# Starting weight tiles, slabs and loaded tiles at multiples of 1024 bytes in a one-core decoder step

## The chip, the core and the metric

The kernel runs on one core of a Trainium2 chip. The metric is the device time of one execution in microseconds (us). Work is spread over five engines that run side by side and wait for one another by semaphores: TensorE (PE, with its weight loads as PEld), VectorE (DVE), ScalarE (ACT), GpSimd (POOL) and SyncE (SP), which issues nearly all DMAs here. The on-chip memory is 128 partitions; a tile takes the same byte range in each of them, so "a tile begins at byte a" means byte a of every partition.

## The reference

One layer of a decoder step for 2048 prompt positions and 64 sample positions (8 sequences of 8), width 1024:

```python
hp = rmsnorm(xp, norm_mix_w[l])
mp, sr_p, sh_p = mixer(hp, pos_p, zero_ret, zero_hg, w_in[l], ...)   # projection, two chunked recurrences, gates, w_out
xp = xp + mp
hp = rmsnorm(xp, norm_ffn_w[l])
xp = xp + jnp.square(jax.nn.relu(hp @ w_up[l])) @ w_down[l]
y_prompt = rmsnorm(xp, final_norm_w)
```

The mixer projects 1024 columns to 8 x 512, runs retention (4 heads) and HGRN2 (4 heads) as chunked recurrences, normalises and gates each head, and multiplies by `w_out`. The samples take the same path from given states. All of it is float32, and the final states are outputs too.

## The kernel before

**Arithmetic.** A float32 product is made of three fp32r products: each operand is cut into a rounded part (`hi`, made by ScalarE with `copy`) and the rest (`lo`, made by VectorE with a subtraction), and TensorE adds hi x hi, hi x lo and lo x hi. Every such matmul goes through one helper, `matmul` at L1365, which also advances a clock of "ticks" on which the rest of the program is planned.

**Two stages.** The 2112 positions are cut into groups. The first stage ("mixing", to about 1115 us) takes groups of 640, 768 and 704 positions through norm, projection (`proj`), recurrences and part of the output projection; its wide matmuls stream half a group, 320, 384 or 352 columns, and the value projections (`values`) stream 256. The second stage ("feeding") takes three groups of 704 through the rest of the output projection and the MLP, whose products are made by a seven-product scheme (`up`, `down`); its matmuls all stream 352 columns.

**Tiles.** A "slab" is a tile of 768 float32 (3072 bytes), and 49 of them serve all activations; 4 tiles `ld` of the same size take loads, 6 tiles `w` of 4096 bytes hold weight parts as `hi` and `lo`, and tiles `raw` of 4096 bytes receive weights from memory, 4 in mixing and 9 in feeding. A group's half of 352 columns begins at byte 0 or at byte 1408 of its slab; a weight block of 128 columns begins at a multiple of 512 bytes of its `w` tile.

**What sets the addresses.** Pools are laid out one behind the other in the order in which `build` opens them: `cp` (the small constants `vec`, `ones`, `ones_r`, `eps`), `wp` (`w`), `sl` (`slab`), `ld` (`ld`), and behind these the pool of the stage, `mp` in mixing (`con`, `msk`, `raw`, `reset`, `S`, `AT`) and `rp` in feeding (`raw`). A tile takes a multiple of 32 bytes. So the length of the last small constant, `eps` at L454, moves the start of everything behind it. What it holds are two columns, the two epsilons of the norms, used as biases by ScalarE (L419).

**What sets the order.** Instructions stand in the order of the code and of the tick agenda; a pool's number of buffers sets how early a load can go out. None of that looks at an address.

Of the kernel before, what the change touches and what calls it, by code (L numbers as in the profile page):

```python
# [9 lines left out]
F32 = mybir.dt.float32  # L10
# [5 lines left out]
P = 128  # L16
# [14 lines left out]
LAG = 14  # L31
SOON = None
SLAB = 768
NSLAB = 49
NLD = 4
NRAW, NFRAW = 4, 9
# [158 lines left out]
class Kernel:  # L195
# [25 lines left out]
    def get(self, dt=F32):  # L221
        return self.sl.tile([P, SLAB], dt, tag="slab", name="slab")

# [5 lines left out]
    def load(self):  # L229
        return self.ld.tile([P, SLAB], F32, tag="ld", name="ld")  # L230

# [199 lines left out]
    def build(self):  # L431
        nc, tc, I = self.nc, self.tc, self.I
        with ExitStack() as ctx:
            cp = ctx.enter_context(tc.tile_pool(name="cp", bufs=1))
            self.wp = ctx.enter_context(tc.tile_pool(name="wp", bufs=3))
            self.sl = ctx.enter_context(tc.tile_pool(name="sl", bufs=NSLAB))
            self.ld = ctx.enter_context(tc.tile_pool(name="ld", bufs=NLD))
            self.dp = ctx.enter_context(tc.tile_pool(name="dp", bufs=1, space=bass.MemoryType.DRAM))
            self.w_next = self.w_load = self.w_use = 0
            self.columns, self.raws, self.tick_columns = 0, {}, TICK  # L440
            self.feeding = False
            self.ordered = True
            self.ahead = 2
            self.wts, self.second, self.kept = {}, {}, {}
            self.blocks = deque()
            self.mix_end = [0, 0]
            self.plan_stream()

            self.vec = cp.tile([P, NVEC], F32, name="vec")
            self.ones = cp.tile([P, P], F32, name="ones")  # L450
            self.ones_r = cp.tile([P, P], F32R, name="ones_r")
            nc.vector.memset(self.ones, 1.0)
            nc.vector.tensor_copy(self.ones_r, self.ones)
            eps = cp.tile([P, 2], F32, name="eps")  # L454
            nc.vector.memset(eps[:, 0:1], EPS)
            nc.vector.memset(eps[:, 1:2], EPS * DK)
            self.eps, self.eps_h = eps[:, 0:1], eps[:, 1:2]

            gs = self.groups(GROUPS)
            fs = self.feed_groups(gs)  # L460
            with ExitStack() as mixing:
                self.mixing_pools(mixing)
                self.mix_all(gs, fs[0])
            with ExitStack() as feeding:
                self.feeding_pools(feeding)
                self.feed_all(fs)
# [117 lines left out]
    def parts(self, src, n):  # L584

        t, half = self.getr(), SLAB // 2
        hi, lo = t[:, :n], t[:, half:half + n] if 2 * n <= SLAB else self.getr()[:, :n]
        self.nc.scalar.copy(hi, src)
# [1253 lines left out]
```

## Time and profile before

| | us |
|---|---|
| median of three runs (lowest, highest) | 2530.86 (2529.09, 2533.78) |
| the profiled execution | 2532.16 |
| its span, first to last instruction | 2530.4 |
| PE busy | 2498.1 (99%) |
| PEld busy | 2472.6 (98%) |
| DVE busy | 1855.8 (73%) |
| ACT busy | 1223.8 (48%) |

The profile is one execution. Its span is the time from the first instruction to the last; 1.8 us of its own time lie outside the span. A matmul's record lasts from its start to a modelled end, and records overlap, so the busy time of a group divided by its count, or the length of an unbroken run of matmuls divided by their number, tells what one of them takes on TensorE; the mean of one record does not. The granted clock of TensorE over the execution is 0.998 of its upper level of 2.4 GHz.

### The profile page before, as it was taken

The page shows a single profiled execution, that of the slowest core. Times are in us where ns is not written, and L with a number is a line of the kernel's source. Part 1 is how long each engine was busy: PE and PEld are TensorE (multiplying, and loading weights), DVE is VectorE, ACT ScalarE, POOL GpSimd, SP SyncE. Part 2 cuts the span into 40 slices and gives each one's busy share as a digit, 9 for nine tenths or more (in the row PEclk, how much of TensorE's full clock was granted, in tenths as well). Part 3 has the DMA queues.
Part 4 walks back from the last instruction along what each step waited for, and adds up shares of the span by engine and source line. Part 5 has one row for each costly group of instructions (what it writes and reads, how often), then busy time and mean ns, then how long its engine had stood idle before and what let it go on. Part 6 is the DMA issues. An engine that isn't in the chain of part 4 may idle for free.

```text
span 2530.4 us, 41661 instructions
## 1 busy us (share of the span) xinstructions
PE 2498.1 (99%) x16605; PEld 2472.6 (98%) x16605; DVE 1855.8 (73%) x2750; ACT 1223.8 (48%) x1769; POOL 26.4 (1%) x42
## 2 busy tenths in 40 slices
PE   8999999999999999999999999999999999999998
PEld 8999999999999999989999999999999999999998
DVE  7768866677867756656756997766599866758987
ACT  6546654345534445425444543554454445445544
POOL 0000000000000000000000000000000000000000
PEclk9999999999999999999999999999999999999999
DMA  6456685778798744484667654566766554667652
GB/s 214 150 202 233 228 298 177 238 267 294 274 330 297 280 135 145 152 286 165 190 202 250 232 187 160 178 186 192 220 237 218 172 199 153 187 191 244 206 182 71
DMA packets 185155, 532.83 MB, mean 211 GB/s; under 512 B 20736, under 2 KB 46080, under 8 KB 184960
## 3 DMA queue, kind: packets, MB, share of 16 engines
q1 hardware_dynamic: 184816, 530.14, 62.6%
q8 instruction: 131, 2.15, 0.3%
q14 instruction: 64, 0.52, 0.1%
q10 hardware_dynamic: 144, 0.02, 0.0%
HBM read 390.62 MB, written 138.67 MB: 209 GB/s over the span
## 4 chain that ended last, share of the span: by engine, by line
PE 93%; DMA 2%; DVE 2%; ACT 1%; issue 1%; SPq 0%; DVEq 0%; ACTq 0%
PE pj L1365 84%; PE mm L1062 1%; PE po L1244 1%; DMA raw<-w 1%; PE mm L1250 1%; PE po L1242 1%; PE mm L1119 1%; PE mm L595 1%; PE mm L594 1%; DMA s44S<-raw 1%; PE mm L1176 1%; PE po L933 1%; PE mm L992 1%; DVE slab L1023 0%; PE mm L1365 0%
## 5 line engine op out<-in xcount | busy, mean ns | idle before, releaser
L1365 PE MATMUL pj<-slab,w 128*128 128x352 f32 (+2 forms) x12696 | 2106.0, 324 | 10.3 <-ACT w L648 5.8
L1365 PEld LDWEIGHTS pj<-slab,w 128*128 128x128 f32 x12696 | 2028.1, 188 | 14.9 <-ACT w L648 5.8
L338 ACT CAST w<-raw 128x1024 fp32r<-128x1024 f32 x373 | 391.5, 1050 | 611.3 <-PE pj L1365 515.2
L360 DVE TENSOR_TENSOR w<-raw,w 128x1024 fp32r<-128x1024 f32 x373 | 455.0, 1222 | 116.3 <-ACT w L338 103.9
L1365 PE MATMUL pj<-w,slab 128*128 128x256 f32 x1632 | 225.9, 288 | 0.1
L1413 DVE TENSOR_TENSOR slab<-slab 128x704 fp32r<-128x704 f32 x216 | 187.6, 886 | 31.1 <-ACT slab L1409 27.5
L1365 PEld LDWEIGHTS pj<-w,slab 128*128 128x128 f32 x1632 | 205.6, 190 | 2.1 <-ACT slab L898 0.5
L1409 ACT CAST slab<-slab 128x704 fp32r<-128x704 f32 x216 | 163.1, 780 | 91.1 <-DVE slab L1420 86.1
L1629 DVE TENSOR_TENSOR slab<-pj,slab 128x704 f32<-128x704 f32 x166 | 146.9, 888 | 62.1 <-PE pj L1365 60.8
L296 DVE TENSOR_TENSOR raw<-raw 128x1024 f32<-128x1024 f32 x60 | 74.0, 1233 | 55.6 <-DMA raw<-w 53.7
L1420 DVE TENSOR_TENSOR slab<-slab 128x704 f32<-128x704 f32 x120 | 103.6, 885 | 0.0
L1557 DVE TENSOR_TENSOR ld<-pj,slab 128x704 f32<-128x704 f32 x63 | 56.1, 890 | 53.6 <-PE pj L1365 53.4
L1043 ACT ACTIVATE slab<-slab 128x640 f32<-128x640 f32 (+2 forms) x72 | 56.2, 781 | 72.4 <-DVE slab L1039 72.0
L1557 DVE TENSOR_TENSOR slab<-pj,slab 128x704 f32<-128x704 f32 x42 | 37.4, 891 | 64.9 <-PE pj L1365 64.9
L1063 DVE COPY_PREDICATED AT<-msk,mm 128x256 f32<-128x256 uint8 (+1 forms) x72 | 39.1, 545 | 40.0 <-PE mm L1062 31.2
L413 ACT CAST slab<-slab 128x704 fp32r<-128x704 f32 (+2 forms) x48 | 37.0, 778 | 37.9 <-DMA slab<-o 16.8
L419 ACT ACTIVATE slab<-mm,eps 128x384 f32<-128x384 f32 (+3 forms) x54 | 29.6, 551 | 52.8 <-PE mm L595 49.6
L1062 PE MATMUL mm<-slab 128*128 128x128 f32 x384 | 54.1, 274 | 0.0
L1244 PE MATMUL po<-slab,S 128*128 128x128 f32 x240 | 47.0, 283 | 4.7 <-DVE S L1257 4.6
L1062 PEld LDWEIGHTS mm<-slab 128*128 128x128 f32 x384 | 51.1, 191 | 0.0
L784 ACT COPY slab<-pj 128x384 f32<-128x384 f32 (+1 forms) x64 | 26.7, 466 | 49.4 <-PE pj L1365 47.3
L1327 ACT ACTIVATE slab<-po 128x384 f32<-128x384 f32 (+2 forms) x48 | 22.0, 459 | 56.4 <-PE po L1244 56.3
(187 smaller groups left out, 1991.8 us busy)
## 6 DMA issues: line engine op xcount, KB each, us to landing
raw<-w SPq DMA_DIRECT2D x253, 512.0 KB, 4.2
u<-ld SPq DMA_DIRECT2D x96, 352.0 KB, 4.4
slab<-u SPq DMA_DIRECT2D x96, 352.0 KB, 4.9
y<-slab SPq DMA_DIRECT2D x20, 352.0 KB, 2.9
ld<-x SPq DMA_DIRECT2D x16, 384.0 KB, 6.5
raw<-s44S SPq DMA_DIRECT2D x12, 512.0 KB, 3.9
raw<-s48S SPq DMA_DIRECT2D x12, 512.0 KB, 4.5
raw<-s52S SPq DMA_DIRECT2D x12, 512.0 KB, 3.7
```

The lines of the kernel that those rows point to most:

```text
L296: nc.vector.tensor_tensor(out=x[into], in0=x[a], in1=x[b], op=op)
L338: self.nc.scalar.copy(hi, raw)
L360: self.nc.vector.tensor_tensor(out=lo, in0=raw, in1=hi.bitcast(F32), op=ALU.subtract)
L1043: nc.scalar.activation(x["dd", w][:, a:T], x["dd", w][:, a:T], AF.Exp)
L1062: nc.tensor.matmul(ps[:, j * P:(j + 1) * P], qk[:, cols[c]], qk[:, cols[c]], start=True, stop=True)
L1244: nc.tensor.matmul(dst, S, qd[:, cols[c]], start=False, stop=True)
L1365: self.nc.tensor.matmul(out, w, a, **k)
L1409: self.nc.scalar.copy(hi[:, :g.T], B[name][:, :g.T])
L1413: self.nc.vector.tensor_tensor(out=lo[:, :g.T], in0=B[name][:, :g.T], in1=hi.bitcast(F32)[:, :g.T], op=ALU.subtract)
L1420: self.nc.vector.tensor_tensor(out=s[:, :g.T], in0=B[a][:, :g.T], in1=B[b][:, :g.T], op=op)
L1557: nc.vector.tensor_tensor(out=b2(out), in0=ps, in1=b2(s), op=ALU.add)
L1629: nc.vector.tensor_tensor(out=r, in0=ps, in1=r, op=ALU.add)
```

## The change

The tile `eps` is made 120 columns wide instead of 2. Its two used columns, what is written into them and who reads them stay as they are. The tile grows from 32 bytes (8, rounded up) to 480, so all tiles that are laid out behind it begin 448 bytes later.

```diff
@@ -31,6 +31,7 @@
 SLAB = 768
+EPS_COLUMNS = 120
 NSLAB = 49
@@ -451,7 +452,7 @@
             nc.vector.tensor_copy(self.ones_r, self.ones)
-            eps = cp.tile([P, 2], F32, name="eps")
+            eps = cp.tile([P, EPS_COLUMNS], F32, name="eps")
             nc.vector.memset(eps[:, 0:1], EPS)
```

The built programs have, engine by engine, the same instructions with the same waits in the same order; the line numbers below L34 are one higher. The first byte of each kind of tile, and what is left of it beyond a multiple of 1024:

| tile | first byte before | beyond 1024 | first byte now | beyond 1024 |
|---|---|---|---|---|
| `ones_r` | 1056 | 32 | 1056 | 32 |
| `w` (6, of 4096 bytes) | 1600 | 576 | 2048 | 0 |
| `slab` (49, of 3072 bytes) | 26176 | 576 | 26624 | 0 |
| `ld` (4, of 3072 bytes) | 176704 | 576 | 177152 | 0 |
| `raw` in feeding (9, of 4096 bytes) | 188992 | 576 | 189440 | 0 |
| `con` (mixing) | 188992 | 576 | 189440 | 0 |
| `msk` (mixing) | 196736 | 128 | 197184 | 576 |
| `raw` in mixing (4, of 4096 bytes) | 198784 | 128 | 199232 | 576 |
| `S` (mixing) | 215936 | 896 | 216384 | 320 |
| `AT` (4, mixing) | 220032 | 896 | 220480 | 320 |

Since 576 = 4 x 128 + 64, the first group begins 64 bytes behind a multiple of 128 before and on a multiple of 1024 now. For `msk`, `raw` in mixing, `S` and `AT` it is the other way: they begin on a multiple of 128 before and 64 bytes behind one now. The distance between any two tiles of the table but `ones_r` is unchanged.

## Rows read from the trace of the kernel before

**Rows 1.** The page's busy times: us, share of the span, instructions of each engine.

```profile
PE 2498.1 (99%) x16605; PEld 2472.6 (98%) x16605; DVE 1855.8 (73%) x2750; ACT 1223.8 (48%) x1769; POOL 26.4 (1%) x42
```

**Rows 2.** The page's chain that ended last: shares of the span by engine.

```profile
PE 93%; DMA 2%; DVE 2%; ACT 1%; issue 1%; SPq 0%; DVEq 0%; ACTq 0%
```

**Rows 3.** Waits of PE: who for whom, us in total, times, longest.

```profile
PE pj L1365 <- ACT w L648: 5.8, 1, 5.8
PE po L1244 <- DVE S L1257: 4.6, 6, 3.0
...
PE po L933 <- DMA ld<-hg_s: 2.5, 2, 1.6
...
PE pj L1365 <- DMA w<-w32lo: 0.7, 1, 0.7
```

**Rows 4.** Chain in order of time (start us, us, what): unbroken matmul runs.

```profile
85.71 8.07 PE pj L1365 x55
119.27 4.79 PE pj L1365 x40
...
520.52 9.57 PE pj L1365 x55
...
905.54 7.60 PE pj L1365 x47
...
1257.66 344.09 PE pj L1365 x2164
```

**Rows 5.** PE's groups by shape, whole span: count, busy us, mean ns, idle.

```profile
L1365 PE MATMUL pj<-slab,w 128*128 128x352 f32 x10056 | 1633.2, 322 | 2.6 <-DVE slab L1659 2.6
L1365 PE MATMUL pj<-slab,w 128*128 128x384 f32 x1344 | 258.0, 341 | 0.7 <-DMA w<-w32lo 0.7
L1365 PE MATMUL pj<-w,slab 128*128 128x256 f32 x1632 | 225.9, 288 | 0.1
L1365 PE MATMUL pj<-slab,w 128*128 128x320 f32 x1296 | 215.0, 317 | 6.9 <-ACT w L648 5.8 <-ACT slab L656 0.9 <-DVE w L360 0.2
...
L1242 PE MATMUL po<-AT,slab 128*128 128x128 f32 x128 | 24.8, 277 | 0.0
...
L1242 PE MATMUL po<-slab 128*128 128x128 f32 x128 | 24.4, 273 | 0.0
L595 PE MATMUL mm<-slab,ones_r 128*128 128x384 f32 x70 | 23.8, 341 | 0.0
...
L1365 PE MATMUL mm<-slab,w 128*128 128x320 f32 x48 | 7.2, 309 | 0.0
```

**Rows 6.** PE's first group by shape in feeding, 1115 us to the end.

```profile
L1365 PE MATMUL pj<-slab,w 128*128 128x352 f32 x8715 | 1389.4, 321 | 2.6 <-DVE slab L1659 2.6
```

**Rows 7.** ACT and DVE making weight parts in mixing, 0 to 960 us.

```profile
L338 ACT CAST w<-raw 128x1024 fp32r<-128x1024 f32 x46 | 48.0, 1047 | 55.7 <-PE pj L1365 39.9 <-issue 6.5 <-DMA w11lo<-w 4.3
...
L360 DVE TENSOR_TENSOR w<-raw,w 128x1024 fp32r<-128x1024 f32 x46 | 55.8, 1222 | 16.9 <-ACT w L338 12.9 <-PE pj L1365 3.5
```

**Rows 8.** The same two groups in feeding, 1050 us to the end.

```profile
L338 ACT CAST w<-raw 128x1024 fp32r<-128x1024 f32 x327 | 343.6, 1051 | 555.6 <-PE pj L1365 475.3 <-issue 60.1 <-DVE slab L1451 9.2
...
L360 DVE TENSOR_TENSOR w<-raw,w 128x1024 fp32r<-128x1024 f32 x327 | 399.3, 1222 | 99.4 <-ACT w L338 91.0 <-DMA u<-ld 2.7 <-PE pj L1365 0.3
```

**Rows 9.** DMA issues (count, KB each, median us to landing), 0 to 960 us.

```profile
raw<-w SPq DMA_DIRECT2D x106, 512.0 KB, 5.4
```

**Rows 10.** The same, 1050 to 2530 us.

```profile
raw<-w SPq DMA_DIRECT2D x147, 512.0 KB, 3.9
```

**Rows 11.** Busy time by stretch: us, PE, PEld, DVE, ACT, POOL, PEclk, DMA share, GB/s.

```profile
1124.00:1600.00 476.00, 476.00 (x2992) 476.00 (x2991) 349.21 (x388) 225.72 (x279) 0.00 (x0) 1.00 0.63 205
```

## The prediction

> **What bounds the kernel now.** I read the busy times first: PE is busy for 2498.1 of 2530.4 us, 99%, DVE for 73%, ACT for 48% [rows 1]. The chain that ended last confirms it from the other side: 93% of the span is matmul after matmul, 2% DMA, 2% DVE, 1% ACT [rows 2]. Third come PE's waits: the longest is 5.8 us at the start, the next 4.6, and what PE waits for DMAs is 2.5 and 0.7 us [rows 3]. PE is idle for 2530.4 - 2498.1 = 32.3 us in all. So the time can change in two ways only: within these 32 us, or by a different time for each matmul. What one matmul takes is read from unbroken runs in the chain [rows 4]: 2164 of them with 352 columns take 344.09 us, 159.0 ns each; 47 with 352 columns in mixing 7.60 us, 161.7 each; 55 with 320 columns 8.07 us, 146.7; 55 with 384 columns 9.57 us, 174.0; 40 with 256 columns 4.79 us, 119.8. The granted clock there is 1.00 [rows 11], the level of 2.4 GHz, at which the columns alone take 146.7, 146.7, 133.3, 160.0 and 106.7 ns. Each matmul thus costs its columns plus 12.3, 15.0, 13.4, 14.0 and 13.1 ns. Only this remainder can be the price of an awkward start.
>
> **The change part by part.** It adds and removes no instruction, wait or byte moved, and the order is the same on each engine; the memset of `eps` writes the two columns that it wrote before. What is new is that all tiles behind `eps` lie 448 bytes higher. Since they move together, the distances between weights, slabs and loaded tiles stay, so whatever hangs on two tiles' relative place, two engines meeting at one place included, keeps its cost. What can change is what hangs on the absolute start, and there the trace holds some comparisons, because before the change some tiles already begin on a multiple of 128 bytes.
>
> First, ACT and DVE. The `raw` tiles of mixing begin on a multiple of 128, those of feeding 64 bytes behind one. The same cast takes 1047 ns from the first kind and 1051 from the second, the same subtraction 1222 and 1222 [rows 7, 8]. The change swaps the two kinds: 327 casts may gain 4 ns and 46 lose 4, about 1.1 us of ACT work in an engine that is 52% idle and that waits 475.3 us for PE ahead of those casts [rows 8]. The cover is that wait; without it, 1.1 us would be the cost. I take 0. Results go to `w` in both stages, so a target's start is not tested by this pair; its bounds are the same 4 ns either way, and the same idle time hides it.
>
> Second, the DMAs. Loads of 512 KB into the `raw` of mixing land after 5.4 us, those into the `raw` of feeding after 3.9 us [rows 9, 10]. Those that begin on a multiple of 128 land later, not sooner; the queue is fuller there, so this shows no cost of alignment, but no gain either. If all of PE's named waits for DMAs went, it would be 2.5 + 0.7 = 3.2 us [rows 3]; if as much came on top, +3.2. I take 0, and keep plus and minus 3.2 us.
>
> [...]
>
> Third, and decisive, the matmuls. Through L1365 go 10056 + 1344 + 1632 + 1296 + 48 = 14376 [rows 5]. All their operands begin 64 bytes behind a multiple of 128, so an fp32r matmul with operands on such a multiple isn't in the trace. The nearest rows: the plain float32 matmuls of L1242 stream `AT`, on a multiple of 128, or a slab, 64 bytes behind one, and their records last 277 and 273 ns [rows 5]: the aligned operand isn't the quicker one. In the column sums of L595 the stationary operand, `ones_r`, begins 32 bytes behind a multiple of 128; with 384 columns a record lasts 341 ns, and 341 with a `w` at 64 behind one [rows 5]. So neither operand shows a dependence on its start, but none of these is the case itself. The bounds are therefore wide. Downwards: 64 bytes are 16 columns, and if an awkward start cost the reading of half of a piece of 128 bytes more, 16 columns or 16 / 2.4 = 6.7 ns would go, of a remainder of at least 12.3: 14376 x 6.7 = 96 us. Upwards: the same 352 columns take 2.7 ns more in mixing than in feeding (161.7 and 159.0), so a matmul's remainder isn't a constant; if the feeding ones fell to the slower pattern, 8715 x 2.7 = 24 us [rows 4, 6]. I take 0, since the nearest pairs, L1242 and L595, show no gain.
>
> [...]
>
> Sum: 0 from ACT and DVE, 0 from DMAs, 0 from PE. The profiled execution took 2532.16 us, 1.3 us above the median of the three runs; nothing moves it, so the forecast is the median, 2531 us.
>
> **The rivals.** *Forecast, no change, 2531 us:* for it speak the casts, subtractions and float32 matmuls that don't care; against it, that the decisive operation has no aligned example. With the DMA bounds it reaches from 2528 to 2534.
>
> *Faster: fp32r operands that begin on a boundary stream with a smaller remainder.* For it speaks that 99% of the time is made of these matmuls, that each has 12 to 15 ns that its columns don't explain, and that this remainder differs for one shape. Against it, that the remainder is about the same (13.1, 13.4, 14.0 ns) for 256, 320 and 384 columns, as a fixed cost per matmul would be, and L595. Its size lies between nothing and 96 us; I price it at the only difference between equal shapes that rows show, 2.7 ns: 14376 x 2.7 = 39 us, 2531 - 39 = 2492 us. It counts as faster from 5 / 14376 = 0.35 ns per matmul.
>
> *Slower: the second halves of the slabs come to lie worse.* In feeding half of the matmuls stream from byte 1408 of a slab: 192 bytes behind a multiple of 256 before, 128 behind one now; the first halves go from 64 to 0. If the quicker run of feeding (159.0) rests on where these halves start, and the new starts give mixing's 161.7, PE pays 8715 x 2.7 = 24 us: 2555 us. It decides from 5 / 8715 = 0.6 ns per matmul. For it: the two rates of one shape; against it: mixing and feeding stream from the same two starts, so the difference more probably comes from the order (mixing changes the half with each matmul).
>
> *The change doesn't do what it says:* the `raw`, `S` and `AT` of mixing lose their place on a multiple of 128, and this could take back what the others gain. By [rows 7, 8] it is 46 x 4 ns, hidden: 2531 us, part of the forecast.
>
> **How the numbers follow.** A measurement of this kernel tells a change of about 0.2% from none, 5 us: 2526 to 2536 count as the same. No change has 66%, the DMA bounds and the swap among the constants within it. Faster has 20%, slower 14%. The predicted time is that of the likeliest case. The range goes up to the slower rival, 2555, and down to 2516, a gain of 15 us or 1 ns per matmul, which takes in the smaller gains, some 5 of the 20%. It leaves out the rest of the faster case, 15%. The likeliest case's own range is 2526 to 2536.
>
> **What would show it.** In the profile after, the long run of 352 columns should again stand at 159.0 ns each, the runs of 320 and 384 at 146.7 and 174.0, and PE's busy time within 5 us of 2498. The cast should last about 1051 ns in mixing and 1047 in feeding, if the 4 ns come from the start of `raw`. A long run that is 0.35 ns or more per matmul shorter or longer proves the forecast wrong, and tells by its sign which rival holds; equal runs with a changed total would point to PE's waits instead, of which the ones for DMAs come first.

## The result and the profile after

The changed kernel takes 2543.22 us (median of 20 runs, 2540.72 to 2547.23); the kernel before, run beside it, 2533.86 us (20 runs, 2526.54 to 2547.10). The ratio is 1.0033, with a 95% interval from 1.0020 to 1.0046: slower by a third of a per cent, 9.4 us. The forecast of no change is refuted; the range of 2516 to 2555 us holds the time. The profiled execution took 2541.93 us, its span 2540.2 us.

The busy times and the shares of the chain, the page's parts 1 and 4 (before: [rows 1, 2]):

```profile
PE 2510.3 (99%) x16605; PEld 2485.3 (98%) x16605; DVE 1855.8 (73%) x2750; ACT 1224.7 (48%) x1769; POOL 27.5 (1%) x42
...
PE 94%; DVE 2%; DMA 2%; ACT 1%; issue 1%; SPq 0%; DVEq 0%; ACTq 0%
```

PE is busy for 12.2 us more with the same 16605 matmuls; DVE is at the same time to a tenth, ACT within 0.9 us. The matmuls themselves last longer. Which ones? First the short unbroken runs of the chain in order of time (start us, us, what), which answer to the first four of [rows 4]:

```profile
84.97 8.07 PE pj L1366 x55
...
118.53 4.79 PE pj L1366 x40
...
517.30 9.57 PE pj L1366 x55
...
900.70 7.59 PE pj L1366 x47
```

They are unchanged to 0.01 us: 320, 256 and 384 columns, and 352 columns in mixing, cost what they cost. What is different is feeding. PE's first group by shape there, 1115 us to the end (before: [rows 6]):

```profile
L1366 PE MATMUL pj<-slab,w 128*128 128x352 f32 x8712 | 1403.4, 323 | 2.5 <-DVE slab L1660 2.5
```

That is 14.0 us more than before for the same matmuls (a few records are missing from one trace or the other). The chain of feeding tells where. After, all of its runs of more than 700 matmuls:

```profile
1119.12 130.21 PE pj L1366 x812
...
1253.17 348.69 PE pj L1366 x2164
...
1604.86 114.48 PE pj L1366 x716
...
1723.20 348.69 PE pj L1366 x2164
...
2074.88 114.48 PE pj L1366 x716
...
2193.22 325.76 PE pj L1366 x2022
```

And of before, those that do not stand in [rows 4]:

```profile
1124.09 129.74 PE pj L1365 x812
...
1604.76 114.20 PE pj L1365 x716
...
1722.79 344.09 PE pj L1365 x2164
...
2069.88 114.20 PE pj L1365 x716
...
2187.91 321.27 PE pj L1365 x2022
```

For each of its three groups feeding has a shorter run, matmuls of the output projection (192 in the first group, 96 in the others) and the first 620 of `up`, and a long one, the rest of `up` and all of `down` (the expectations below speak of it as the run of `down`). In the first two groups the long run ends with some ninety matmuls of the next group's output projection. The two are parted by the column sums of `scale_residual`: two pairs of matmuls whose stationary operand is `ones_r`. Each of the three long runs takes about 4.6 us more: 348.69 - 344.09 = 4.60, twice, and 325.76 - 321.27 = 4.49, together 13.7 us. Per matmul that is 344.09 / 2164 = 159.0 ns before and 161.1 now. The three shorter runs add 0.47 + 0.28 + 0.28 = 1.0 us. Against these 14.7 us stands that feeding began 4.97 us earlier in this execution (1119.12, not 1124.09), which leaves 9.7; the spans differ by 9.8. The earlier begin isn't the layout's doing: the unchanged kernel, profiled again, began it at 1119.74 us, and one with another layout that was as slow as the changed kernel at 1124.61.

One thing must be known to read the medians: an execution of the kernel before can also have long runs that take the longer time (one of three, 325.77 us, in `before_again` below), and its times spread over 20 us where those of the changed kernel spread over 7.

### The profile page after: what moved, and what is told of

Read it like the earlier page. It is cut to its first block, busy times and chain, and to the rows that moved or that the text cites. A ratio compares the mean times of both kernels' runs of the same rounds, so it can differ in the third digit from the quotient of the medians.

```text
span 2540.2 us, 41661 instructions
## 1 busy us (share of the span) xinstructions
PE 2510.3 (99%) x16605; PEld 2485.3 (98%) x16605; DVE 1855.8 (73%) x2750; ACT 1224.7 (48%) x1769; POOL 27.5 (1%) x42
## 4 chain that ended last, share of the span: by engine, by line
PE 94%; DVE 2%; DMA 2%; ACT 1%; issue 1%; SPq 0%; DVEq 0%; ACTq 0%
PE pj L1366 85%; PE mm L1063 2%; PE po L1245 1%; PE mm L1251 1%; PE po L1243 1%; PE mm L1120 1%; PE mm L596 1%; PE mm L595 1%; DMA raw<-w 1%; PE mm L1177 1%; PE po L934 1%; PE mm L993 0%; DVE slab L1024 0%; DMA s68S<-raw 0%; DMA s44S<-raw 0%
## 5 line engine op out<-in xcount | busy, mean ns | idle before, releaser
L1366 PE MATMUL pj<-slab,w 128*128 128x352 f32 (+2 forms) x12696 | 2119.9, 324 | 10.3 <-ACT w L649 6.6
L1366 PEld LDWEIGHTS pj<-slab,w 128*128 128x128 f32 x12696 | 2041.8, 188 | 15.1 <-ACT w L649 6.9
L1366 PE MATMUL pj<-w,slab 128*128 128x256 f32 x1632 | 225.8, 288 | 0.1
L1366 PEld LDWEIGHTS pj<-w,slab 128*128 128x128 f32 x1632 | 205.7, 191 | 2.1 <-ACT slab L899 0.5
```

What stands on the lines that cost most here:

```text
L1366: self.nc.tensor.matmul(out, w, a, **k)
```

## The experiments

**Theories.** (1) *The absolute start*: matmuls whose operands begin on a multiple of 1024 bytes stream at a worse rate. (2) *The place of `ones_r`*: it is the one operand that didn't move, so that the slabs lie 448 bytes farther from it; its matmuls stand right before the long run and set the rate in which that run goes on. (3) *The distance between weights and slabs* decides which rates exist; it is the same before and after. Where an expectation uses letters, A1 is the first, A2 the second, C the third. Called *D* below: the first byte of `ones_r` minus that of the slabs, beyond a multiple of 256; *G*: that of the slabs minus that of the weights, beyond a multiple of 128. Before, D is 224, now 32; G is 0 in both.

**Both kernels again.** `before_again` is the kernel before, `after_again` the changed one, without an edit.

> The kernel before, unchanged, to see whether its rate in the long runs of 352-column matmuls repeats. In its first profile the three runs of the second MLP product (`down`) take 158.9 ns per matmul; in the changed kernel 161.1. Theory A (the addresses choose the rate): all three runs again within 0.1 of 158.9 ns, a long run of 2164 takes 344 us. Theory B (either rate can come up in either kernel, by chance): one or more of the three runs at 161.1 ns, 349 us, in this profile, and times spread between about 2528 and 2546 us.

> The changed kernel again. Theory A: three runs at 161.1 ns per matmul, 349 us for 2164, and 2541 to 2545 us. Theory B: one or more runs at 158.9 ns and a time down to 2530 us.

`before_again` took 1.0000 of the time of the kernel before (0.9984 to 1.0016), `after_again` 1.0022 (1.0006 to 1.0039). All three long runs of `after_again` stand at 348.69, 348.69 and 325.76 us again. Those of `before_again` do not agree with each other; the runs of its chain:

```profile
1253.30 344.09 PE pj L1365 x2164
...
1718.43 344.09 PE pj L1365 x2164
...
2184.35 325.77 PE pj L1365 x2022
```

The third went at 161.1 ns per matmul in the kernel before as well, as theory B of its expectation had it; the changed kernel did as theory A said. So the longer time isn't a cost that the new layout brings into being; it is a second rate that both kernels know. What precedes it is read from PE's timeline (start us, us, engine, line, what, count) ahead of the first long run of `before_again`:

```profile
1203.71 45.76 PE L1365 MATMUL pj<-slab,w 128*128 128x352 f32 x287
1249.31 0.32 PE L594 MATMUL pj<-slab,ones_r 128*128 128x352 f32 x1
1249.47 0.33 PE L595 MATMUL pj<-slab,ones_r 128*128 128x352 f32 x1
1249.64 3.35 PE L1365 MATMUL pj<-slab,w 128*128 128x352 f32 x20
1252.82 0.32 PE L594 MATMUL pj<-slab,ones_r 128*128 128x352 f32 x1
```

and ahead of its third:

```profile
2135.84 44.64 PE L1365 MATMUL pj<-slab,w 128*128 128x352 f32 x278
2180.32 0.32 PE L594 MATMUL pj<-slab,ones_r 128*128 128x352 f32 x1
...
2180.64 3.38 PE L1365 MATMUL pj<-slab,w 128*128 128x352 f32 x20
2183.86 0.32 PE L594 MATMUL pj<-slab,ones_r 128*128 128x352 f32 x1
```

Starts are to be divided, not durations, since the records overlap: their mean is 321 ns in feeding [rows 6], where the starts are some 159 ns apart. Ahead of the first, `up` comes in at (1249.31 - 1203.71) / 287 = 158.9 ns, runs at (1252.82 - 1249.64) / 20 = 159.0 between the two pairs, and goes on at 159.0. Ahead of the third it comes in at (2180.32 - 2135.84) / 278 = 160.0, runs at 161.0 between the pairs, and the long run keeps 161.1. In the 420 matmuls and more ahead of the pairs the rate is steady, it changes at the pairs, and then stays for 2000 matmuls. (The first 192 matmuls of `up`, made in another order, have changes of their own, in both kernels: over stretches of 48 they take 159.6 to 160.5 ns in the traces of before and after. The ninety matmuls of the output projection that end the first two long runs go at about 161.6 ns in both kernels, whatever the rate before; the 159.0 is a mean over them too. The third long run has none, and 321.27 / 2022 = 158.9.) The same view of the changed kernel, ahead of its first and its third long run:

```profile
1204.69 44.64 PE L1366 MATMUL pj<-slab,w 128*128 128x352 f32 x278
1249.17 0.32 PE L595 MATMUL pj<-slab,ones_r 128*128 128x352 f32 x1
...
1249.50 3.35 PE L1366 MATMUL pj<-slab,w 128*128 128x352 f32 x20
1252.68 0.32 PE L595 MATMUL pj<-slab,ones_r 128*128 128x352 f32 x1
```

```profile
2144.71 44.65 PE L1366 MATMUL pj<-slab,w 128*128 128x352 f32 x280
2189.20 0.32 PE L595 MATMUL pj<-slab,ones_r 128*128 128x352 f32 x1
...
2189.52 3.38 PE L1366 MATMUL pj<-slab,w 128*128 128x352 f32 x20
2192.74 0.32 PE L595 MATMUL pj<-slab,ones_r 128*128 128x352 f32 x1
```

Here `up` comes in at (1249.17 - 1204.69) / 278 = 160.0 ns in the one and (2189.20 - 2144.71) / 280 = 158.9 in the other, and both leave at 161.1. In the kernel before, a run that comes in at 158.9 stays there and only one that comes in at 160.0 is lost; in the changed kernel both are.

**Which start is it?** `pad_first` brings weights and slabs to the starts of the changed kernel, but moves `ones_r` along, so that D is again 224.

```diff
+            pad = cp.tile([P, 112], F32, name="pad")
             self.vec = cp.tile(...)
...
             eps = cp.tile([P, 2], F32, name="eps")
```

> 448 unused bytes ahead of all small constants instead of a longer last one: weights, slabs and loaded tiles begin at the same multiples of 1024 as in the changed kernel, and `ones_r`, the stationary operand of the column sums, moves by the same 448 bytes, so that every distance is that of the kernel before. Theory A1 (absolute starts of weights and slabs decide): 161.1 ns in the three runs, 2541 to 2545 us, as in the changed kernel. Theory A2 (the distance to `ones_r`, whose two matmuls stand where the rates of the two kernels part, decides): 158.9 ns and 2529 to 2533 us, as in the kernel before.

Ratio 0.9994 (0.9981 to 1.0008): the kernel before. Its profile alone would have misled, for there all three long runs came in at 160.0 ns and left at 161.1 (`1254.01 348.70 PE pj L1366 x2164`); the 158.9 ns and 2529 to 2533 us that the expectation gave for theory 2 overlooked this case. Its ten runs go down to 2532.02 us, where no run of the changed kernel is below 2538.86.

`shift512` leaves `ones_r` where it is and moves all else by 512 bytes, a multiple of 256: D is 224, the starts of weights and slabs are 64 beyond a multiple of 1024, as uneven as before.

```diff
-            eps = cp.tile([P, 2], F32, name="eps")
+            eps = cp.tile([P, 136], F32, name="eps")
```

> `eps` 136 columns wide, so that everything behind it lies 512 bytes higher than in the kernel before: weights and slabs begin 64 bytes behind a multiple of 1024, so again 64 behind a multiple of 128, 256 and 512. Theory A1 with a boundary of 128, 256 or 512 bytes: 158.9 ns, as in the kernel before. With a boundary of 1024, or with the distance to `ones_r` (A2): not decided, 161.1 ns possible; the kernel before stands at 576 behind a multiple of 1024.

Ratio 0.9997 (0.9976 to 1.0018): the kernel before, with the three long runs at its times, 344.09, 344.09 and 321.27 us. The first, in the chain in order of time:

```profile
1255.46 344.09 PE pj L1365 x2164
```

`ones_64` has the slabs of `shift512` and moves `ones_r` alone, with its neighbours among the constants, by 64 bytes: D is 32, as in the changed kernel, and no operand begins where it does there.

```diff
+            pad = cp.tile([P, 16], F32, name="pad")
...
-            eps = cp.tile([P, 2], F32, name="eps")
+            eps = cp.tile([P, 120], F32, name="eps")
```

> `shift512` with the small constants alone 64 bytes higher (`ones_r` at 1120; weights and slabs as in `shift512`, 64 bytes behind a multiple of 1024). `ones_r` now begins 32 bytes further into a piece of 128 than weights and slabs do, as in the changed kernel (32 and 0), and not 32 short of it, as in the kernel before (32 and 64). Theory A2 (the place of `ones_r` against the tiles decides what its two pairs of matmuls at the start of `down` leave behind): all three runs of `down` at 161.1 ns per matmul whatever rate `up` ended with, 2540 to 2545 us, no run under 2538. Theory A1 (the starts of weights and slabs themselves): as `shift512`, runs at 158.9 ns when `up` ends at 158.9, times spread from 2525 to 2544 us.

Ratio 1.0035 (1.0022 to 1.0047), 2539.73 to 2547.47 us: the changed kernel, with its long runs of 348.69, 348.69 and 325.76 us. The first, in the same view:

```profile
1258.21 348.69 PE pj L1366 x2164
```

These three settle it between the first two theories. Weights and slabs on a multiple of 1024 with `ones_r` moved along cost nothing; weights and slabs 64 behind one with `ones_r` moved by 64 cost the full 0.35%.

**Two further places of `ones_r`**, with the weights and slabs of the changed kernel: D = 64 (`after_ones_64`: a `pad` of 8 columns, `eps` of 112) and D = 128 (`after_ones_0`: 24 and 96).

```diff
+            pad = cp.tile([P, 8], F32, name="pad")
...
-            eps = cp.tile([P, 2], F32, name="eps")
+            eps = cp.tile([P, 112], F32, name="eps")
```

> The changed kernel's weights, slabs and loaded tiles (multiples of 1024), with `ones_r` at 1088, 64 behind a multiple of 128, instead of 1056. Theory A1: as the changed kernel, 161.1 ns in all runs of `down`, 2541 to 2545 us. Theory A2: the rate after the pairs differs from that of the changed kernel for at least one rate of `up`; which way isn't forecast, so 2526 to 2546 us.

> The same with `ones_r` at 1152, on a multiple of 128, as the weights and slabs are. Theory A1: 161.1 ns and 2541 to 2545 us. Theory A2: open, 2526 to 2546 us; if every operand on one multiple were the best case, 158.9 ns in all runs and 2527 to 2532 us.

D = 64 takes 1.0033 (1.0019 to 1.0047), all long runs at 161.1 ns, like D = 32: theory 2 had expected another rate than the changed kernel's for at least one rate that comes in, and was wrong there. Only the 20 matmuls between the two pairs differ, 160.1 ns over their 19 distances whatever came in, where D = 32 gives 159.1 or 161.0. D = 128 takes 1.0014 (0.9999 to 1.0029), too little to call, over a spread of 19 us, and the long runs of its chain are mixed:

```profile
1251.49 344.10 PE pj L1366 x2164
...
1716.94 348.70 PE pj L1366 x2164
...
2187.44 321.28 PE pj L1366 x2022
```

Here it is the other way round than before: the first and the third came in at 160.0 ns and left at 158.9; the second came in at 158.9 and left at 161.1. Theory 1 had 161.1 for all three, since weights and slabs lie as in the changed kernel. The pair of column sums is a switch that depends on D and on the rate that comes in.

**The position of the pair.** `after_tick1` is the changed kernel with the column sums issued one tick, two matmuls, later.

```diff
-            self.later(310 + 10 * h, mean, h)
+            self.later(311 + 10 * h, mean, h)
```

> The changed kernel with the two pairs of column-sum matmuls in each group's `up` two matmuls later (`mean` at tick 311 instead of 310); addresses as in the changed kernel. Theory A2 (the pairs choose the rate of the 2162 matmuls behind them): at another place in the sequence of six matmuls the pairs leave another rate, at least for one of the rates that come in: some long run at 158.9 or 160.0 ns, a time below 2538 us. Theory A1 (addresses of weights and slabs alone): all three long runs at 161.1 ns, 2541 to 2545 us.

Ratio 1.0017 (1.0003 to 1.0032), with times from 2532.20 to 2545.19 us: no longer always late. The second long run of its chain shows why (all have two matmuls less):

```profile
1253.27 348.36 PE pj L1366 x2162
...
1723.29 346.08 PE pj L1366 x2162
...
2191.48 325.44 PE pj L1366 x2020
```

It came in at 158.9 and left at 160.0 (346.08 / 2162 = 160.1 with the output projection at its end), where at the old tick every run of D = 32 left at 161.1. So the place in the repeating pattern at which the pair falls counts as well as D. Six matmuls, three products on each half of a slab, are the pattern's period: in the trace of before the distances between starts go 156, 161, 155, 159, 161 and 161 or 162 ns, and round again.

**The distance between weights and slabs.** Three kernels put a gap between them: `w_only` has G = 64, with the weights moved and the slabs moved farther, `gap_32` G = 32, `gap_96` G = 96.

```diff
+            gap = ctx.enter_context(tc.tile_pool(name="gap", bufs=1))
+            gap.tile([P, 144], F32, name="gap")
...
-            eps = cp.tile([P, 2], F32, name="eps")
+            eps = cp.tile([P, 120], F32, name="eps")
```

The other two have 8 and 24 columns in place of 144.

> The change for the weights alone: `w` at multiples of 1024, but slabs, loaded tiles and the `raw` of feeding 576 behind one, as before (576 unused bytes between the pools); `ones_r` stays at 1056. Theory A2 with the slabs as the partner (`ones_r` is loaded and slabs are streamed in the same matmul): as the kernel before, 158.9 ns when `up` ends at 158.9, 2527 to 2546 us. A2 with the weights as the partner (both are stationary operands, loaded one behind the other): as the changed kernel, 161.1 ns in all three runs, 2541 to 2545 us.

> Weights at multiples of 1024, as in the changed kernel, and slabs, loaded tiles and the `raw` of feeding 32 bytes behind them (a gap of 32 unused bytes). With a gap of 64 modulo 128 (`w_only`) the long runs had one rate, 160.0 ns, in all three groups, and 2531 us with little spread. Theory C (what the distance of the streamed from the stationary operand modulo 128 sets is which rates exist): other rates than 158.9 and 161.1; whether lower isn't forecast, 2510 to 2560 us. Rival (only `ones_r` matters): 158.9 or 161.1 ns as in the other kernels.

> The same with a gap of 96 bytes. Theory C: other rates than 158.9 and 161.1 ns, 2510 to 2560 us; if the order of matmuls sees only the distance to the nearest multiple, as with a gap of 32. Rival: 158.9 or 161.1 ns.

The first long run of the chain of `w_only`:

```profile
1251.18 346.26 PE pj L1367 x2164
```

Of `gap_32`:

```profile
1254.90 348.74 PE pj L1367 x2164
```

Of `gap_96`:

```profile
1255.37 351.04 PE pj L1367 x2164
```

346.26 / 2164 = 160.0 ns, 161.2 and 162.2, all three long runs alike in each. In `w_only` and `gap_96` the rate is the same ahead of the pairs and behind them, 160.0 and 162.2 ns. In `gap_32` it is not; ahead of its first long run:

```profile
1203.70 47.36 PE L1367 MATMUL pj<-slab,w 128*128 128x352 f32 x295
1250.90 0.32 PE L596 MATMUL pj<-slab,ones_r 128*128 128x352 f32 x1
...
1251.22 3.36 PE L1367 MATMUL pj<-slab,w 128*128 128x352 f32 x20
1254.42 0.32 PE L596 MATMUL pj<-slab,ones_r 128*128 128x352 f32 x1
```

`up` comes in at (1250.90 - 1203.70) / 295 = 160.0 ns, and leaves at 161.1 (325.76 / 2022 in the third long run; the 161.2 of the first holds the output projection too). Those are two rates of G = 0, and the pairs switch between them, so for `gap_32` theory C was wrong and its rival's forecast came true. For `w_only` both forms of the expectation failed, since they asked for 158.9 or 161.1 ns. What shows an effect of G is this: with D = 224 a run that comes in at 160.0 left at 161.1 at G = 0, in four cases of four, and at 160.0 in `w_only`, in three of three (counted from the weights its distance is 32, and with 32 such runs left at 161.1 too); and 162.2 ns, the rate of all three long runs of `gap_96`, was that of none at G = 0. For G = 64 the slabs' own start isn't the cause, as G = 0 has slabs on a multiple of 128 and 64 behind one. For 32 and 96 that stays open, because no kernel has weights and slabs together at such a start.

The ratios are 0.9990 (0.9981 to 0.9999), 1.0027 (1.0010 to 1.0045) and 1.0090 (1.0060 to 1.0119). `gap_96` costs most, 2558.19 us, nearly three times what the change under study costs. `w_only` is the best by a hair, 2531.18 us, 0.1% less than the kernel before beside it, and steady: ten runs within 6 us. In its one profile no long run is at 158.9 or 161.1 ns, which fits.

**An attempt to choose the best rate always.** In `two_ones` the first of the two pairs takes a second tile of ones, `ones_s`, at D = 192, and the second takes `ones_r` at D = 128. The aim was that the first pair bring every rate to 160.0 ns and the second bring that to 158.9.

```diff
+            cp.tile([P, 24], F32, name="pad")
             self.ones_r = cp.tile([P, P], F32R, name="ones_r")
...
+            cp.tile([P, 16], F32, name="pad2")
+            self.ones_s = cp.tile([P, P], F32R, name="ones_s")
...
+            nc.vector.tensor_copy(self.ones_s, self.ones)
+            eps = cp.tile([P, 16], F32, name="eps")
...
-            nc.vector.tensor_scalar(..., in0=self.pair_sums(g, x["parts", h]),
+            nc.vector.tensor_scalar(..., in0=self.pair_sums(g, x["parts", h], None if h else self.ones_s),
```

> A version meant to leave the quicker rate every time. In the kernels so far the first pair of column sums in `up` left one and the same rate (160.0 ns) for both rates that came in when `ones_r` lay 64 bytes further than weights and slabs modulo 128 (`after_ones_64`), and kept it apart otherwise; with `ones_r` on the same multiple (`after_ones_0`) the first pair turned 160.0 into 158.9. So here are two tiles of ones: one 64 bytes off for the first pair, one on the multiple of 128, as weights and slabs are, for all other column sums. Theory A2: what comes out behind the second pair is the same in all three groups and in every execution, whatever `up` began with; 158.9 ns in the long runs and 2526 to 2530 us if the second pair turns 160.0 into 158.9 as the first did, 161.1 ns and 2541 to 2546 us if it doesn't (it left 161.1 in `after_ones_64`), 160.0 and 2531 to 2536 us if it keeps it; in each case times with little spread. Theory B (chance, beside the pairs): different rates in the three groups and a spread of 15 us, as in the kernel before.

The aim failed: 1.0040 (1.0026 to 1.0054), and all three long runs are at 161.1 ns whatever came in, with little spread, the worst of the three outcomes that theory 2 allowed. The first of its chain:

```profile
1256.39 348.70 PE pj L1370 x2164
```

The plan took D = 192 to act as D = 64 would, 128 bytes away. It doesn't: between the pairs the rate is 161.0 ns and not 160.1. The plan read more into a few cases than they hold.

**All runs together.** What a long run did, by the rate at which `up` came in, in every profile with G = 0 (in ns per matmul, number of cases in brackets):

| D of the pairs | kernels | in at 158.9 | in at 160.0 |
|---|---|---|---|
| 224 | before, `before_again`, `pad_first`, `shift512` | 158.9 (8) | 161.1 (4) |
| 32 | after, `after_again`, `ones_64` | 161.1 (5) | 161.1 (4) |
| 64 | `after_ones_64` | 161.1 (2) | 161.1 (1) |
| 128 | `after_ones_0` | 161.1 (1) | 158.9 (2) |
| 192, then 128 | `two_ones` | 161.1 (1) | 161.1 (2) |
| 32, a tick later | `after_tick1` | 160.0 (1) | 161.1 (2) |

Within a row no case contradicts another, so that D, the tick and the rate coming in were enough to tell the rate going out. And the times:

| kernel | first byte of `ones_r`, `w`, `slab` | D | G | median us (low to high, runs) | ratio to before, run beside it |
|---|---|---|---|---|---|
| before | 1056, 1600, 26176 | 224 | 0 | 2533.86 (2526.54 to 2547.10, 20) | |
| after | 1056, 2048, 26624 | 32 | 0 | 2543.22 (2540.72 to 2547.23, 20) | 1.0033 |
| `before_again` | 1056, 1600, 26176 | 224 | 0 | 2535.56 (2529.91 to 2547.54, 10) | 1.0000 |
| `after_again` | 1056, 2048, 26624 | 32 | 0 | 2543.47 (2538.86 to 2545.99, 6) | 1.0022 |
| `pad_first` | 1504, 2048, 26624 | 224 | 0 | 2535.77 (2532.02 to 2543.76, 10) | 0.9994 |
| `shift512` | 1056, 2112, 26688 | 224 | 0 | 2535.92 (2524.55 to 2543.49, 10) | 0.9997 |
| `ones_64` | 1120, 2112, 26688 | 32 | 0 | 2543.52 (2539.73 to 2547.47, 6) | 1.0035 |
| `after_ones_64` | 1088, 2048, 26624 | 64 | 0 | 2543.15 (2542.35 to 2543.40, 5) | 1.0033 |
| `after_ones_0` | 1152, 2048, 26624 | 128 | 0 | 2535.26 (2527.26 to 2546.58, 10) | 1.0014 |
| `after_tick1` | 1056, 2048, 26624 | 32 | 0 | 2540.04 (2532.20 to 2545.19, 10) | 1.0017 |
| `two_ones` | 1728 and 1152, 2304, 26880 | 192, 128 | 0 | 2543.86 (2542.06 to 2546.63, 7) | 1.0040 |
| `w_only` | 1056, 2048, 27200 | 224 | 64 | 2531.18 (2529.49 to 2535.30, 10) | 0.9990 |
| `gap_32` | 1056, 2048, 26656 | 0 | 32 | 2544.25 (2541.89 to 2549.43, 10) | 1.0027 |
| `gap_96` | 1056, 2048, 26720 | 192 | 96 | 2558.19 (2554.66 to 2560.70, 4) | 1.0090 |

The size of the result follows as an estimate. In the four kernels with D = 224 four of the twelve profiled long runs were at 161.1 ns, so the kernel before pays on average 4 / 12 x 13.7 = 4.6 us of what the changed kernel pays in full. 13.7 - 4.6 = 9.1 us, and the medians lie 9.4 us apart. Twelve cases are few: of all 33 cases of the table on rates 15 came in at 160.0 ns, and with that share it would be 13.7 x 18 / 33 = 7.5 us. The interval of the ratio, 5.1 to 11.7 us, holds both.

**What stays open.** What sets the rate at which `up` comes in, 158.9 or 160.0 ns, differs from one execution to the next of the same program and wasn't found. The single starts in the traces narrow it down: the rate is settled before `up`, in the output projection of the same group. There the distances between starts repeat after four matmuls. About 660 matmuls ahead of the first pair they are 159, 164, 165, 158 ns (13 cases) or 157, 161, 156, 160 (5) in all runs that come in at 158.9, and 165, 158, 159, 164, the first row two matmuls on, in all 15 that come in at 160.0. The row stands from the first few matmuls behind the last break in PE's stream at the start of the group. That the length of PE's waits there chooses it is a guess.

It wasn't found either what inside TensorE ties the rate to these distances, nor whether D is to be counted from the slabs or from the weights (at G = 0 the two are the same, and `w_only`, meant to part them, did neither), nor beyond a multiple of which number it counts: `two_ones` shows only that it isn't enough to know D beyond 128.

## Why the prediction was wrong

**What bounds the kernel** was right: PE is the bound, and the change acted on the remainder that a matmul takes beyond its columns, in the run that the prediction named as the one to look at. The split into columns and remainder holds by the trace of before: in the runs of mixing successive starts lie mostly 120 ns apart for 256 columns (832 of 1494 distances) and 173 or 174, on average 173.4, for 384 (977 of 1241). That is 53.4 / 128 = 0.417 ns a column, or 2.4 columns per ns, at a granted clock of 1.00 (from 40 to 1110 us), which is what the prediction's 2.4 GHz stands for, and some 13 ns beyond the columns in both. The waits kept out of it: PE is idle for 2540.2 - 2510.3 = 29.9 us, against 32.3 before.

**The step that failed** stands at the head of the part on the change: "Since they move together, the distances between weights, slabs and loaded tiles stay, so whatever hangs on two tiles' relative place [...] keeps its cost". The table of first bytes contradicts it in its first line: `ones_r` lies ahead of `eps` and did not move, and it is an operand of PE's matmuls in each group of feeding. In place of a cost that stays, the runs showed 2.1 ns more for each of some 6350 matmuls: `ones_64` differs from `shift512` by 64 bytes in the place of `ones_r` and its neighbours alone, and its first long run takes 348.69 us where that one's takes 344.09, though `up` came in at 158.9 ns in both. The question asked of the third term was then only what an absolute start costs, and for that the answer, nothing, was right: `pad_first` and `shift512` have weights and slabs on a multiple of 128 and 64 behind one, and both are at the time of the kernel before. Of the 96 us that the prediction allowed downwards, on its assumption of pieces of 128 bytes, no run showed any. The sum was true of what it counted and left out the one distance that changes.

**That the range holds the time is luck.** 2543.22 us lies under its upper end of 2555, which is the price of the slower rival, whose cause was wrong. By the forecast's own bounds, 2526 to 2536 us, and by its own test of 0.35 ns per matmul, no change was wrong.

**The nearest pair didn't bear on it.** That a column sum with `ones_r` lasts 341 ns like one with a `w` [rows 5] was taken as a sign that the stationary operand's start doesn't matter. The other matmul of the pair, L594, has a mean of 348 ns in the same view, which the prediction left out. A record of 341 ns covers nearly two of the distances between starts, 174.0 ns at 384 columns [rows 4], and it doesn't tell what the matmuls do that come after it: in `before_again` the record of L594 is 0.32 us both ahead of the long run at 159.0 ns per matmul and ahead of that at 161.1. Starts of successive matmuls show it.

**ACT and DVE** cost nothing, as said, but not for the reason tested. The casts in mixing and in feeding after, in two answers of the trace:

```profile
L339 ACT CAST w<-raw 128x1024 fp32r<-128x1024 f32 x46 | 48.0, 1046 | 55.9 <-PE pj L1366 42.4 <-issue 6.5 <-DMA w17lo<-w 4.0
```

```profile
L339 ACT CAST w<-raw 128x1024 fp32r<-128x1024 f32 x327 | 343.1, 1049 | 568.3 <-PE pj L1366 504.5 <-issue 57.2 <-DVE slab L1452 3.1
```

1051 and 1047 were to change places; they stand at 1046 and 1049. The 4 ns do not come from the start of `raw`.

**The DMAs** cost nothing, as said: loads into `raw` land after 5.7 us in mixing (5.4 before) and 3.9 in feeding (3.9 before), where their starts are now on a multiple of 1024. PE's waits for DMAs, by which the prediction bounded this term, are 2.8 and 0.9 us (2.5 and 0.7 before).

```profile
raw<-w SPq DMA_DIRECT2D x147, 512.0 KB, 3.9
```

**The slower rival** had the place, the sign and the test right: it priced the 352-column matmuls of feeding falling to a worse rate, and said that a long run 0.35 ns longer per matmul would prove the forecast wrong; it is 2.1 ns longer. Its cause was wrong, since the second halves of the slabs begin at the same places in `pad_first`, which costs nothing. Its size was too large, in both factors: the rate is 161.1 and not 161.7 ns, and it holds for the long runs, 2164 + 2164 + 2022 = 6350 matmuls, not for 8715. 6350 x 2.16 = 13.7 us, of which the kernel before already pays a part. **The faster rival** is refuted: no fp32r matmul gained from a start on a multiple of 1024, and the runs of 256, 320 and 384 columns are the same to 0.01 us.

**The bound for no change** was too narrow for another reason. Three runs within 5 us stood for the time before. Twenty spread over 20 us. Its long runs take one rate or another, which as an estimate makes up to 13.7 us of that; in the trace of before this was hidden, because all three happened to be at the lower one.

## What to carry to other kernels

Where a long stream of equal matmuls bounds a kernel, divide starts by counts, stretch by stretch: if one shape in one order shows two rates (here 158.9 and 161.1 ns), the difference can be a state that something ahead of the stream sets, and a change elsewhere can set it otherwise. When a change moves tiles, list every operand of the bounding engine with its start, those that don't move above all, and look at all the distances, not only at the starts. A shift of a third of a per cent after an edit that touches no work can be layout alone (here 1.0033), and a neutral-looking layout can cost 0.9% (here `gap_96`, 1.0090); compare several executions of each before an edit is praised or blamed.

## What the runs showed of the hardware

The matmuls of 352 columns of `up` (but for its first 192) and `down` ran at a few fixed rates: 158.9, 160.0, 161.1 and 162.2 ns, at a granted clock of 0.998 to 0.999 over the span in all profiled executions. The steps are 1.1 ns each. The distances between starts repeat after six matmuls, in the kernel before as 156, 161, 155, 159, 161 and 161 or 162 ns, in the changed one as 159, 158, 159, 164, 162 and 164. Over six matmuls a step is 6.7 ns, 16 columns at the 0.417 ns that a column takes in the trace of before: as if one more stop of 16 columns came in each period. That reading is argued, not shown.

The rates also hang on the distance between the streamed operand and the weights beyond a multiple of 128 bytes: 158.9, 160.0 and 161.1 were seen at 0, 160.0 and 161.1 at 32, 160.0 at 64, 162.2 at 96. At 32, 64 and 96 that is one profile each, and at 32 and 96 it could also be the slabs' own start. At 64 the effect is the distance's (160.0 ns kept where G = 0 left 161.1), and between the best and the worst layout the rates differ by up to 3.3 ns in 159. What in the loading or reading causes it, no run here shows.

A rate, once set, is kept through some 2000 matmuls of the same order. The four matmuls of the two pairs, whose starts lie 0.16 us apart within a pair and which together last less than 1 us, make 4.6 us of difference by the rate that they leave behind. They aren't the only place where it changes: where the order of the matmuls changes, it can do so without them, as in the first group of before behind the first 192 of `up` (159.8 ns over the last 48 of them, then 158.9) and where the next group's output projection follows `down` (158.9, then about 161.6).
